# A copy moved ahead of a subtraction, and idle products between the first transposes

## The chip, the cores and the metric

The kernel runs on one core of a Trainium2 chip. A core has five engines with a queue of instructions each: TensorE (PE in the profile; its weight loads are listed apart as PEld) multiplies matrices, VectorE (DVE) and ScalarE (ACT) work on elements, GpSimd (POOL) does little here, and SyncE (SP) issues most DMA transfers. Products land in PSUM, which has eight banks of 128x512 float32; everything else that engines read lies in SBUF. The metric is the device time of one launch in microseconds (us). Less is better.

## The reference, cut to what matters

The program is a trunk of two layers over 1024 tokens of width 1024. Layer 0 mixes tokens with a gated MLP and a gated delta rule, layer 1 with differential attention; after each comes an MLP and a gated embedding. Only the first lines matter here:

```
hn = rms_norm(h, ln_mix_e[i])        # h is x at first
proj = hn @ w_in_e[i]
```

The norm divides each token's row by its root mean square and multiplies each of the 1024 columns by a gain, `ln_mix_e`. The product with `w_in_e` is the first product of the program.

## The kernel before

All activations are kept transposed: 128 columns of the model (one k of eight) by 512 tokens (one half of the sequence). A product in float32 is made of three in a faster 32-bit type: each operand is split into a high part (`hi`, the rounded value) and a low part (`lo`, the rest), and hi\*hi, lo\*hi and hi\*lo are summed in one PSUM bank.

For the first half of x the work before the first product is this:

- SyncE and ScalarE issue the loads: ScalarE first the gain's 8x128 values (L2063), then two pieces of x (L2050); SyncE, in turn, four pieces of each of x's two tiles and the pieces of the first weight (L103). A tile of x holds two blocks of 128 tokens; a piece is 256 of its columns, 256 KB, enough for two values of k. The loads use eight completion slots in turn, so the ninth is issued when the first slot's load has landed.
- TensorE runs five products of the identity with itself whose result nobody reads (`idle`, L2061, recorded at L78). Then it transposes the gain (into `pt`) and x, four 128x128 blocks for each k (recorded at L81), into a PSUM bank of 512 columns.
- ScalarE casts a weight piece to its high part (L226), and VectorE subtracts to get the low part (L227). Each weight piece of 256 rows becomes one 128x512 tile pair.
- VectorE copies the transposed gain from PSUM to `cols` (L2067). With it ScalarE evicts a transposed k as `hi` (L234) and VectorE makes `lo` (L235).
- `keep` copies the transposed x again, to `xt` (L880), and stores it to `h_dram` for the residual sum. `squares` (L885) is eight ScalarE instructions that sum x\*x by rows, for the norm. The division by the root mean square is done later, on the product's result.

The order on each engine's queue is fixed when the program is built: a planner replays the program against its own estimates of time and places each instruction; marks added by `Ordered.behind` only restrict that order. On the chip each queue then runs strictly as it was laid down. So an edit at the start also moves other instructions, by the planner's choice.

PSUM has two banks for each of the names `mm`, `aux`, `tr` and `sc`. Before the change the transposes of k take `aux`, `tr`, `sc` in turn, the idle products `tr`, the gain `aux`, and the first products `mm`.

Of the kernel before, what the change touches and what calls it, by code (L numbers as in the profile page):

```python
# [14 lines left out]
ALU = mybir.AluOpType  # L15
# [3 lines left out]
P = 128  # L19
# [4 lines left out]
HT = 512  # L24
# [8 lines left out]
MARKS = ((64, 50), (192, 144), (223, 168))  # L33
TAIL = 220
FILLA, FILLB, FILLC, FILLD = 62, 36, 28, 29
IDLE = 5

SYSTEMS = "k0 k1,k2 k3 d0,d1 s0,d2 s1 k4,d3 s2 k5,s3 k6 k7 d4,d5 s4,d6 s5,d7 s6,s7,,,,,".split(",")
FILLS = (20, 20, 20, 20, 26, 26, 28, 28)
# [2 lines left out]
def f32(ap):  # L42
    return ap.bitcast(F32)


class Ordered:
# [3 lines left out]
    def __init__(self, tc):  # L50
        self.tc, self.engine = tc, tc.nc.tensor
        self.fill = False
        self.start(0)
# [30 lines left out]
class Weight:  # L84
# [8 lines left out]
    def split(self, upto=None):  # L93
        while len(self.tiles) < min(upto or self.pieces, self.pieces):
            if len(self.raws) == len(self.tiles):
                self.load()
            self.tiles.append(self.T.parts(self.raws[len(self.tiles)], self.lo_engine))
# [19 lines left out]
class Trunk:  # L117
# [3 lines left out]
    def __init__(self, tc, ctx):  # L121
        self.tc, self.nc = tc, tc.nc
        nc = self.nc
        self.cp = ctx.enter_context(tc.tile_pool(name="const", bufs=1))
        self.wp = ctx.enter_context(tc.tile_pool(name="w", bufs=2))
        self.hp = ctx.enter_context(tc.tile_pool(name="hs", bufs=1))
        self.tp = ctx.enter_context(tc.tile_pool(name="tmp", bufs=TB))
        self.sp = ctx.enter_context(tc.tile_pool(name="small", bufs=2))

        self.rp = ctx.enter_context(tc.tile_pool(name="region", bufs=1))  # L130
        self.ps = ctx.enter_context(tc.tile_pool(name="ps", bufs=2, space=PSUM))
        self.wide = ("mm",)
        self.dp = ctx.enter_context(tc.tile_pool(name="dram", bufs=1, space=DRAM))
        self.n = self.turn = 0
        self.pe = Ordered(tc)
        self.ident = self.cp.tile([P, P], F32, name="ident")
        make_identity(nc, self.ident)
        self.ones = self.cp.tile([P, 1], F32, name="ones")
        nc.vector.memset(self.ones, 1.0)
        self.mhalf = self.cp.tile([P, 16], F32, name="mhalf")  # L140
        nc.vector.memset(self.mhalf, -0.5)

        warm = self.cp.tile([P, 1], F32, name="warm")
        nc.scalar.activation(warm, self.ones, AF.Tanh)
        self.hs = [None, None]

    def nm(self, s):
        self.n += 1
        return f"{s}_{self.n}"
# [74 lines left out]

    def split(self, src, hi, lo, lo_engine=None):
        self.nc.scalar.copy(hi, src)  # L226
        self.split_mark = (lo_engine or self.nc.vector).tensor_tensor(lo, src, f32(hi), ALU.subtract).ins.name  # L227
        return hi, lo

    def put_h(self, k, half, h, gain):  # L230
# [639 lines left out]
        self.pe.floor = None  # L870


    def load_x(self, rows, half, gain, h_dram):
        nc = self.nc
        ss = self.sp.tile([P, 2, 4], F32, tag="ssx", name=self.nm("ssx"))
        junk = self.slot("B", [P, 2, HT], F32, "junk")

        def keep(k, ps):
            xt = self.slot(f"c{k % 4}", [P, HT], F32, "xt")
            (nc.vector.tensor_copy if k % 4 else nc.scalar.copy)(xt, ps)  # L880
            nc.sync.dma_start(h_dram[k, :, half * HT : (half + 1) * HT], xt)

        def squares(i, u):
            for t in (2 * u, 2 * u + 1):
                inst = nc.scalar.activation(junk[:, t % 2], rows[t][:, i * HT : (i + 1) * HT], AF.Square, accum_out=ss[:, i, t : t + 1])  # L885
                if not half:
                    self.pe.behind(inst, marks[3 + 4 * i])

        late, marks = [], []
        for k in range(KT):  # L890

            ps = self.aux([P, HT], "aux" if half else ("aux", "tr", "sc")[k % 3], "aux")
            for t in range(4):
                self.pe.transpose(ps[:, t * P : (t + 1) * P], rows[t][:, k * P : (k + 1) * P], self.ident)
            marks.append(self.pe.mark)
            self.put_h(k, half, ps, gain[:, k : k + 1])
            late.append((k, ps))
            if half:
                keep(*late.pop())
                if k % 4 > 1:  # L900
                    squares(k // 4, k % 2)
            elif k > 3:
                keep(*late.pop(0))
            yield
        with contextlib.nullcontext() if half else self.tc.high_priority(EARLY):
            for i in range(0 if half else 4):
                squares(i // 2, i % 2)
            ms = self.sp.tile([P, 4], F32, tag="ms", name=self.nm("ms"))
            nc.vector.tensor_tensor(ms, ss[:, 0], ss[:, 1], ALU.add)
            nc.vector.tensor_scalar(ms, ms, 1.0 / D, EPS, ALU.mult, ALU.add)  # L910
            self.take_hs(half, ms)
        while late:
            keep(*late.pop(0))
        yield
# [1117 lines left out]
def trunk(tc, x, p, ln_mix_e, w_in_e, gmlp_v_gain, gmlp_ws, gmlp_bs, gdn_conv, gdn_a_log, gdn_dt_bias, gdn_out_gain,  # L2032
          w_out_e, ln_mix_o, w_qkv_o, attn_q_gain, attn_k_gain, diff_lambda, attn_sub_gain, w_out_o, ln_mlp, w_mlp1,
          w_mlp2, ln_ple, w_ple_gate, w_ple_proj, masks, out):
    with ExitStack() as ctx:
        T = Trunk(tc, ctx)
        nc = tc.nc
# [18 lines left out]
        cols = T.cp.tile([P, P], F32, name="cols")  # L2056
        vr = T.tmp()

        idle = T.aux([P, P], "tr", "idle")
        for _ in range(IDLE):  # L2060
            T.pe.matmul(idle, lhsT=T.ident, rhs=T.ident, start=True, stop=True)  # L2061
        first = Weight(T, [(w_in_e[0][:, 1536:1792], 0)], KT, 256)
        nc.scalar.dma_start(vr[0:8, 0:P], ln_mix_e[0].rearrange("(k p) -> k p", p=P))  # L2063
        x0 = rows(0)
        pt = T.aux_ps()
        T.pe.transpose(pt[:, 0:8], vr[0:8, 0:P], T.ident[0:8, 0:8])
        nc.vector.tensor_copy(cols[:, 0:8], pt[:, 0:8])  # L2067
        gain = [cols[:, i : i + 8] for i in (0, 8, 24, 40, 16, 32)]
        conv = cols[:, 48:96].rearrange("p (t m) -> p t m", m=12)
        lam_init = 0.8 - 0.6 * math.exp(-0.3)  # L2070
# [89 lines left out]
```

## Time and profile before

| what | value |
|---|---|
| time, median of 3 runs | 2512.21 us (2511.91 to 2512.52) |
| time of the profiled execution | 2513.05 us |
| its span, first to last instruction | 2511.1 us |
| busy: PE, DVE, ACT | 2495.5, 1810.3, 1307.4 us |
| first product of x and the weight, start | 9.30 us after the span's start |

In the timeline a row gives the start in us, the time it covers in us, the engine, the line, the operation, the tiles as output<-inputs, the shapes and a count of merged instructions; in brackets the idle time before it and what ended that. Starts count: on TensorE instructions overlap, so the pitch from start to start is what one costs. In the answers by stretch, each engine has its busy time with its count, and PEclk is the share of its clock that TensorE was granted. SPq and ACTq are the queues of those engines, where DMA issues stand.

### The profile page before, as it was taken

The numbers are of one execution on the slowest core, as the hardware profiler recorded it, in microseconds if no ns is written. First come the engines' busy times: TensorE is split into PE (matmuls) and PEld (weight loads), VectorE is DVE, ScalarE is ACT, GpSimd is POOL, SyncE is SP. The second block draws the span as 40 slices with busy tenths as digits, with TensorE's granted clock in tenths as the row PEclk, the third lists the DMA queues.
The fourth block names the chain that finished last, engine by engine and source line by source line (L and its number), as shares of the span: only waits on it lengthen the run. The fifth ranks groups of instructions, "written<-read, shape, count | busy, mean of one in ns | idle before, by whom it ended". The sixth has DMA issues, their size and how long they took to land.

```text
span 2511.1 us, 39815 instructions
## 1 busy us (share of the span) xinstructions
PE 2495.5 (99%) x13903; PEld 2138.6 (85%) x13903; DVE 1810.3 (72%) x3590; ACT 1307.4 (52%) x2654; POOL 258.1 (10%) x221
## 2 busy tenths in 40 slices
PE   9999999999999999999999999999999999999999
PEld 7898998888888888888999999988888888888887
DVE  7768665687666787656577777787887656788576
ACT  6635474554545444544465666655654555445452
POOL 0210220000000000000433333310000000000000
PEclk9999999999999999999999999999999999999999
DMA  7364436467557656544211111147466548666651
GB/s 237 121 187 106 134 114 197 130 194 257 181 173 268 229 175 210 189 130 136 88 46 52 47 43 43 60 142 256 157 217 229 191 164 293 201 187 203 198 176 63
DMA packets 314128, 403.19 MB, mean 161 GB/s; under 512 B 44772, under 2 KB 180936, under 8 KB 313928
## 3 DMA queue, kind: packets, MB, share of 16 engines
q1 hardware_dynamic: 313368, 400.13, 49.5%
q8 instruction: 109, 1.79, 0.3%
q14 instruction: 91, 0.75, 0.1%
q10 hardware_dynamic: 560, 0.53, 0.1%
HBM read 292.02 MB, written 108.53 MB: 160 GB/s over the span
## 4 chain that ended last, share of the span: by engine, by line
PE 95%; DVE 3%; issue 1%; ACT 0%; DMA 0%; POOL 0%; SPq 0%; DVEq 0%; ACTq 0%; POOLq 0%
PE mm L78 83%; PE po L78 3%; PE qk L78 2%; PE aux L78 2%; PE tr L81 2%; DVE lg L1092 0%; DVE t L1452 0%; PE pks L78 0%; PE pkq L78 0%; PE pvn L78 0%; PE aux L81 0%; PE pab L81 0%; DMA x<-in_x_dram 0%; DVE lg L1103 0%; ACT lg L1095 0%
## 5 line engine op out<-in xcount | busy, mean ns | idle before, releaser
L226 ACT CAST w<-raw 128x512 fp32r<-128x512 f32 x598 | 366.7, 618 | 474.9 <-PE mm L78 410.9
L78 PE MATMUL mm<-g,w 128*128 128x512 f32 x2592 | 603.0, 394 | 0.0
L78 PEld LDWEIGHTS mm<-g,w 128*128 128x128 f32 x2592 | 486.4, 188 | 115.5
L78 PE MATMUL mm<-hi,w 128*128 128x512 f32 x1728 | 554.3, 396 | 0.0
L227 DVE TENSOR_TENSOR w<-raw,w 128x512 fp32r<-128x512 f32 x534 | 365.0, 690 | 204.2 <-ACT w L226 190.6
L78 PE MATMUL mm<-w,hi 128*128 128x256 f32 (+2 forms) x2528 | 505.8, 295 | 0.7 <-DVE w L227 0.6
L78 PEld LDWEIGHTS mm<-w,hi 128*128 128x128 f32 x2528 | 400.7, 188 | 14.1 <-DVE w L227 0.8
L78 PEld LDWEIGHTS mm<-hi,w 128*128 128x128 f32 x1728 | 325.1, 189 | 73.4 <-ACT u L375 0.4
L78 PE MATMUL mm<-w,lo 128*128 128x256 f32 (+2 forms) x1264 | 369.6, 293 | 0.0
L78 PE MATMUL mm<-lo,w 128*128 128x512 f32 x864 | 340.7, 395 | 0.0
L78 PE MATMUL mm<-t,w 128*128 128x512 f32 x1152 | 271.7, 394 | 0.0
L78 PEld LDWEIGHTS mm<-t,w 128*128 128x128 f32 x1152 | 216.3, 188 | 51.1
L78 PEld LDWEIGHTS mm<-w,lo 128*128 128x128 f32 x1264 | 238.1, 188 | 5.4
L78 PEld LDWEIGHTS mm<-lo,w 128*128 128x128 f32 x864 | 162.6, 188 | 36.0 <-DVE lo L235 0.2
L264 POOL TENSOR_TENSOR r<-ms,mhalf 128x4 f32<-128x4 f32 x12 | 13.7, 1140 | 1511.0 <-DVE ms L262 1482.7
L227 DVE TENSOR_TENSOR g<-graw,g 128x512 fp32r<-128x512 f32 x216 | 147.4, 684 | 7.3 <-DMA gd<-g 2.8
L226 ACT CAST g<-graw 128x512 fp32r<-128x512 f32 x216 | 132.8, 617 | 26.3 <-DMA gd<-g 13.6
L1095 ACT ACTIVATE lg<-lg,nm 128x128 f32<-128x128 f32 (+7 forms) x128 | 99.4, 777 | 77.0 <-DVE nm L1092 70.3
L359 ACT ACTIVATE g<-g 128x512 f32<-128x512 f32 x100 | 63.0, 630 | 77.6 <-DVE g L293 77.4
L1092 DVE CUSTOM_DVE_ANT_0 lg<-qk,al 128x512 f32<-128x512 f32 (+3 forms) x128 | 74.9, 588 | 33.1 <-PE qk L78 30.3
L227 POOL TENSOR_TENSOR w<-raw,w 128x512 fp32r<-128x512 f32 x64 | 84.4, 1345 | 113.0 <-ACT w L226 64.8
L78 PE MATMUL mm<-ohi,w 128*128 128x512 f32 x256 | 85.2, 400 | 0.5 <-ACT ohi L1149 0.5
(358 smaller groups left out, 3539.1 us busy)
## 6 DMA issues: line engine op xcount, KB each, us to landing
raw<-in_w_mlp_dram SPq DMA_DIRECT2D x352, 256.0 KB, 3.4
graw<-gd SPq DMA_DIRECT2D x224, 256.0 KB, 2.7
gd<-g SPq DMA_DIRECT2D x192, 256.0 KB, 3.4
raw<-in_w_ple_gate_dram SPq DMA_DIRECT2D x76, 256.0 KB, 3.6
acc<-h_dram SPq DMA_DIRECT2D x64, 256.0 KB, 4.4
keep<-in_w_mlp_dram SPq DMA_DIRECT2D x64, 256.0 KB, 4.4
raw<-in_w_in_e_dram SPq DMA_DIRECT2D x60, 256.0 KB, 3.9
h_dram<-acc SPq DMA_DIRECT2D x48, 256.0 KB, 2.8
```

The source lines that it names most:

```text
L78: self._next(self.engine.matmul(*a, **k))
L81: self._next(self.engine.transpose(*a, **k))
L226: self.nc.scalar.copy(hi, src)
L227: self.split_mark = (lo_engine or self.nc.vector).tensor_tensor(lo, src, f32(hi), ALU.subtract).ins.name
L264: nc.gpsimd.tensor_tensor(r, ms, self.mhalf[:, 0:4], ALU.pow)
L359: nc.scalar.activation(g, src, AF.Relu)
L1092: nc.vector.tensor_tensor_reduce(out=lg[:, k0:k1], in0=ps[:, : k1 - k0], in1=al[:, u0 + k0 : u0 + k1], scale=-1.0, scalar=3.0e38 if c == 0 ...
L1095: nc.scalar.activation(lg[:, :n], lg[:, :n], AF.Exp, bias=nm[:, r, nch - 1 : nch], scale=-1.0, accum_out=me.sums[:, b, r : r + 1])
```

## The change

Five edits, all before or at the first product:

1. The copy of the gain to `cols` is named `first_lo`, and the first low part that is made after it in the program must be queued behind it on VectorE.
2. The idle products go from five to six, and write a bank of `sc` in place of `tr`.
3. The transposes of k = 0 and 1 are issued together: both k of x's first tile, five idle products, both k of the second tile, one idle product, and only then the rest.
4. The banks of the transposes are `aux`, `aux`, `tr`, `tr` in turn in place of `aux`, `tr`, `sc`.
5. From k = 4 on, the copy `keep` of k - 4 stands before the transposes of k, since these need its bank.

```
-IDLE = 5
+IDLE = 6
+WAIT = 5, 1
+BANKS = "aux", "aux", "tr", "tr"
...
     def split(self, src, hi, lo, lo_engine=None):
         self.nc.scalar.copy(hi, src)
-        self.split_mark = (lo_engine or self.nc.vector).tensor_tensor(lo, src, f32(hi), ALU.subtract).ins.name
+        inst = (lo_engine or self.nc.vector).tensor_tensor(lo, src, f32(hi), ALU.subtract)
+        if self.first_lo:
+            self.pe.behind(inst, self.first_lo)
+            self.first_lo = None
+        self.split_mark = inst.ins.name
         return hi, lo
...
+    def idle(self, n):
+        for _ in range(n):
+            self.pe.matmul(self.unread, lhsT=self.ident, rhs=self.ident, start=True, stop=True)
...
+        def turn(k, ps, ts):
+            for t in ts:
+                self.pe.transpose(ps[:, t * P : (t + 1) * P], rows[t][:, k * P : (k + 1) * P], self.ident)
+
+        def bank(k):
+            return self.aux([P, HT], "aux" if half else BANKS[k % 4], "aux")
+
+        early = []
+        if not half:
+            early = [bank(0), bank(1)]
+            for ts, n in ((range(2), WAIT[0]), (range(2, 4), WAIT[1])):
+                for k in range(2):
+                    turn(k, early[k], ts)
+                self.pe.floor = self.pe.mark
+                self.idle(n)
+                self.pe.floor = self.pe.mark
         for k in range(KT):
-
-            ps = self.aux([P, HT], "aux" if half else ("aux", "tr", "sc")[k % 3], "aux")
-            for t in range(4):
-                self.pe.transpose(ps[:, t * P : (t + 1) * P], rows[t][:, k * P : (k + 1) * P], self.ident)
+            if early:
+                ps = early.pop(0)
+            else:
+                if not half and k > 3:
+                    keep(*late.pop(0))
+                ps = bank(k)
+                turn(k, ps, range(4))
+                self.pe.floor = None
...
-            elif k > 3:
-                keep(*late.pop(0))
...
-        idle = T.aux([P, P], "tr", "idle")
-        for _ in range(IDLE):
-            T.pe.matmul(idle, lhsT=T.ident, rhs=T.ident, start=True, stop=True)
+        T.unread = T.aux([P, P], "sc", "idle")
+        T.idle(IDLE)
...
-        nc.vector.tensor_copy(cols[:, 0:8], pt[:, 0:8])
+        T.first_lo = nc.vector.tensor_copy(cols[:, 0:8], pt[:, 0:8]).ins.name
```

What the planner makes of it can be read in the built programs. On ScalarE, from the first weight cast on (k is counted from 0; one line is one or more instructions in their order):

```
before: cast piece 0 | hi k0, hi k1 | 2 squares of tile 0 | cast piece 1 | xt k0 | hi k2 | square | hi k3 | square
        | cast piece 2 | square | hi k4 | square | hi k5 | cast piece 3 | hi k6 | square | hi k7 | square | ...
after:  cast piece 0 | 2 squares of tile 0 | cast piece 1 | 2 squares of tile 1 | hi k0, hi k1 | cast piece 2 | hi k2
        | hi k3 | xt k0 | cast piece 3 | casts of the second weight's pieces 0 and 1 | hi k4 | hi k5
        | cast of its piece 2 | 2 squares | hi k6 | 2 squares | cast of its piece 3 | hi k7 | ...
```

The two squares of tile 0 read the columns of its first two pieces, those of tile 1 likewise. On VectorE the copy to `cols` stands before the first low part, and the low part of piece 1 before the first `lo`. On TensorE all transposes of k = 0 to 3 and the idle products stand before the first product, as before; the products of the second weight with k = 0 to 7 (24 of them) are spread between those of the first (48), where they stood behind them, and the first third-weight products come next where before 24 other products of the second came. On SyncE the first stores of `xt` go behind the loads of x's second half. Much later, at the end of the delta rule's solver, some ten groups of instructions change places on TensorE, VectorE and ScalarE; the rest of the program has the same order.

More of the change, by code (lines that the diff above doesn't have):

```diff
@@ L226, in split @@
         self.nc.scalar.copy(hi, src)
-        self.split_mark = (lo_engine or self.nc.vector).tensor_tensor(lo, src, f32(hi), ALU.subtract).ins.name
+        inst = (lo_engine or self.nc.vector).tensor_tensor(lo, src, f32(hi), ALU.subtract)
+        if self.first_lo:
+            self.pe.behind(inst, self.first_lo)
+            self.first_lo = None
+        self.split_mark = inst.ins.name
         return hi, lo
```

## The prediction

> **What bounds the kernel now.** First the page: busy shares and the chain of waits.
>
> ```profile
> span 2511.1 us, 39815 instructions
> PE 2495.5 (99%) x13903; PEld 2138.6 (85%) x13903; DVE 1810.3 (72%) x3590; ACT 1307.4 (52%) x2654; POOL 258.1 (10%) x221
> PE 95%; DVE 3%; issue 1%; ACT 0%; DMA 0%; POOL 0%; SPq 0%; DVEq 0%; ACTq 0%; POOLq 0%
> ```
>
> TensorE is busy for 99% of the span and makes 95% of the chain. So a delay of its first product stays to the end unless a later stall absorbs it, and later stalls are few. Next the chain in order of time over the first 40 us, cut to the start.
>
> ```profile
> 1.81 6.35 DMA x<-in_x_dram
> ...
> 8.20 1.45 PE aux L81 x8
> 9.65 3.10 PE mm L78 x8
> ```
>
> Until 8.2 us the chain waits for x's loads, then runs through transposes into products; from there TensorE never lets go. The change can win or lose only by when products start and how fast they then run. The speed is read from four stretches (busy us with counts for PE, PEld, DVE, ACT, POOL; then PEclk) and the timeline of TensorE.
>
> ```profile
> 2.03:5.44 3.41, 3.14 (x14) 2.37 (x13) 0.36 (x3) 0.91 (x2) 0.00 (x0) 1.00 0.95 219
> 5.44:8.85 3.41, 1.31 (x10) 1.01 (x11) 0.77 (x2) 0.99 (x2) 0.00 (x0) 1.00 1.09 365
> 8.85:12.27 3.42, 3.42 (x12) 2.80 (x11) 2.70 (x4) 3.42 (x9) 0.00 (x0) 0.50 1.10 348
> 12.27:15.68 3.41, 3.41 (x25) 2.94 (x24) 3.10 (x5) 3.41 (x10) 0.00 (x0) 1.00 1.09 365
> ```
> ```profile
> 1.42 2.50 PE L78 MATMUL idle<-ident 128*128 128x128 f32 x10 [1.42 <-POOL ident masks.py:199]
> ...
> 7.18 0.66 PE L81 MATMUL aux<-ident,x 128*128 128x128 f32 x4 [2.02 <-DMA x<-in_x_dram]
> 8.20 1.45 PE L81 MATMUL aux<-ident,x 128*128 128x128 f32 x8 [0.35 <-DMA x<-in_x_dram]
> 9.30 1.20 PE L78 MATMUL mm<-hi,w 128*128 128x512 f32 x2
> 10.30 0.63 PE L78 MATMUL mm<-lo,w 128*128 128x512 f32 x1
> 10.73 0.63 PE L78 MATMUL mm<-hi,w 128*128 128x512 f32 x1
> 11.16 0.63 PE L78 MATMUL mm<-lo,w 128*128 128x512 f32 x1
> ...
> 17.10 0.39 PE L78 MATMUL mm<-lo,w 128*128 128x512 f32 x1
> 17.33 0.39 PE L78 MATMUL mm<-hi,w 128*128 128x512 f32 x1
> ...
> 24.95 1.05 PE L78 MATMUL aux<-ident,r 128*128 128x128 f32 x8
> ```
>
> The granted clock sits at 0.50 from 8.85 to 12.27 and at 1.00 afterwards. At 0.50 products follow at 0.43 us (10.30, 10.73, 11.16), at 1.00 at 0.23 us (17.10, 17.33). The idle products ran at the slow pitch (ten instructions in 2.50 us against eight in 1.05 us at 24.95), so the 1.00 of the first row is no grant, only the absence of a record. The pattern: a stretch with 3.14 of 3.41 us busy is followed by 1.00, one with 1.31 by 0.50, one fully busy by 1.00.
>
> **Edit 1: the gain's copy first.** Three views carry it: VectorE, ScalarE, and three loads from SyncE's queue.
>
> ```profile
> 7.61 0.69 DVE L227 TENSOR_TENSOR w<-raw,w 128x512 fp32r<-128x512 f32 x1 [5.18 <-ACT w L226]
> 8.22 0.16 DVE L2067 COPY cols<-aux 128x8 f32<-128x8 f32 x1
> ```
> ```profile
> 6.96 0.62 ACT L226 CAST w<-raw 128x512 fp32r<-128x512 f32 x1 [4.01 <-DMA raw<-in_w_in_e_dram]
> 8.47 1.27 ACT L234 ACTIVATE hi<-aux,cols 128x512 fp32r<-128x512 f32 x2 [0.90 <-DVE cols L2067]
> 9.63 0.63 ACT L885 ACTIVATE junk<-x 128x512 f32<-128x512 f32 x1
> ...
> 10.24 0.62 ACT L885 ACTIVATE junk<-x 128x512 f32<-128x512 f32 x1
> ...
> 10.86 0.61 ACT L226 CAST w<-raw 128x512 fp32r<-128x512 f32 x1
> 11.36 0.59 ACT L880 COPY xt<-aux 128x512 f32<-128x512 f32 x1
> ```
> ```profile
> 8.17 0.37 SPq L103 DMA_DIRECT2D raw<-in_w_in_e_dram  x1
> 8.64 0.41 SPq L103 DMA_DIRECT2D raw<-in_w_in_e_dram  x1
> 9.39 0.37 SPq L103 DMA_DIRECT2D raw<-in_w_in_e_dram  x1
> ```
>
> Before, the copy waits behind a low part that waits for a load, and ScalarE's first `hi` waits for the copy until 8.47, though its transposes end at 7.85 (7.18 + 0.66). Taken alone, the copy made at about 4.7 us lets `hi` start at 7.9 and saves 0.57 us.
>
> But the built order of ScalarE has something else ahead of `hi`: cast, two squares, cast, two squares. I follow that queue. The first cast ends its issue at about 7.5. The squares read the second piece of x's first tile; that slot is free at 8.17, as SyncE's next issue shows, so they start at about 8.19. Two squares cost 1.23 (9.63 to 10.86 for two): 9.42. The next cast reads weight piece 1, landed by 9.39, so it does not wait: 0.50 (10.86 to 11.36): 9.92. The other tile's piece is there since 8.64; two squares: 11.15. Then `hi` k0 takes 0.69 and the product follows 0.07 later, as before (8.47 + 0.69 = 9.16, weight load 9.23): 11.91 against 9.23. **Later by 2.68 us.** No row suggests that an engine takes its queue out of order: `hi` stood idle behind nothing but its wait before.
>
> **Edits 2 and 3: idle products.** Seven more, two instructions each: 0.43 us each at the slow pitch, 0.22 at the fast. All lie in holes: the sixth delays the gain's transpose by 0.43 us, covered by the wait for x up to 7.18; the five run from about 5.1 to 6.4 (7.3 at worst, 0.1 late for x); the last lies before 8.20. With 11.91 as the start, none reaches the path: cost 0. If the squares did not hold `hi` back, the worst case would be 0.1 to 0.3 us. The new wait (k1's first transpose needs the bank that the gain's copy frees at 4.7) holds only transposes and idle products, all done before 7.2.
>
> Their effect on the clock: the stretch to 5.44 stays busy, so 1.00 holds to 8.85, as before. In 5.44:8.85 about 2.6 us are now busy against 1.31, so 1.00 may hold to 12.27 too, but only 0.36 us of products would use it. In 8.85:12.27 TensorE has the tail of the transposes (to 9.1) and 0.36 us of products: some 0.5 us busy, less than the 1.31 that was followed by 0.50. So 12.27 to 15.68 runs at 0.50. A slow stretch costs the share 1 - 0.23/0.43, or 46%: before 9.23 to 12.27, 3.04 us, 1.40 us lost; now 3.41 us, 1.57 lost. **Later by 0.17 us.**
>
> The Trainium skill (TensorE: Matmul & The Clock Gate, Part 1 and the section on HAM oscillation) says that the clock falls back after a window of about 3.4 us of idleness. The stretch of 5.44:8.85 was busy for 1.31 us and the clock still fell, so the trace asks for less than that; by the page the hole from 9.1 to 11.9 would be too short and the sum would be the first rival's.
>
> **Edits 4 and 5: banks.** With four banks in place of six, k4's transposes wait for ScalarE's `xt` of k0. By the queue: `hi` x2, cast, `hi` x2 from 11.15 (1.17 + 0.50 + 1.17 = 2.84) to 13.99, copy done at 14.6. TensorE comes to them after 14 products: one by 12.27, eight by 15.68, five more: 16.9. Margin 2.3 us, or 0.5 with a fast clock: cost 0. If the margin went, each us would be one us. The later `hi` of k4 (from 15.99 by the same count) is due at 20.9: margin 4.
>
> **Queues passed.** Four loads of x's second half pass the first two stores on SyncE; x comes about a us sooner, and its first transposes did not wait for it before: 0. The stores go later; the residual is read long after: 0. The 24 products of the second weight only change place with the first's: 0, as no operand is due before it is made by the counts above.
>
> **Later moves.** At the end of the solver groups change places, where these stalls lie:
>
> ```profile
> PE pd L78 <- DVE ring L1706: 1.0, 1, 1.0
> PE py L78 <- DVE xts L1796: 0.9, 2, 0.7
> ```
>
> The nearest prices are a stall of 0.7 us gone or one more like it: -0.7 to +0.7. I take 0, as most moves there are swaps of equals.
>
> **The sum:** +2.68 + 0.17 = +2.85 us. Against the profiled execution, 2513.05 us (span 2511.1 and 1.95 around it), 2515.9. That execution lies 0.84 us above the median of the runs shown, 2512.21, so for the median 2515.1.
>
> **The rivals.**
> 1. The clock stays at 1.00 once won. For it: the idle products nearly double the busy time of 5.44:8.85. Against: the hole of 2.8 us behind it. Then the start costs 2.68 and the slow 1.40 is saved: +1.28, 2513.5. The page named above would have it so.
> 2. Two slow stretches after the start, if products that still wait for `lo` don't fill the first. 2.68 + 2 x 1.57 - 1.40 = +4.42, 2516.6. Against: the fully busy 8.85:12.27, which won the clock at once.
> 3. Faster: ScalarE's squares do not hold `hi`, because their pieces and the casts come early enough or the queue runs otherwise. Then the product starts 0.57 sooner and, with the clock kept, 1.40 more is saved: -1.97, 2510.2. It decides if the first `hi` starts before the first square; the built order says no.
> 4. Slower by more than 0.2%: TensorE now reaches the third weight earlier in its order than before, after 72 products, at about 33.0 us (15.68 + 63 x 0.23 + 26 short ones x 0.11). This row shows when its first piece was castable before, after a wait:
>
> ```profile
> 29.16 0.62 ACT L226 CAST w<-raw 128x512 fp32r<-128x512 f32 x1 [1.09 <-DMA raw<-in_w_in_e_dram]
> ```
>
> It is ready at 29.8, 3.2 us ahead. The moved loads and stores would have to make it later by 3.2 + 2.2 us before the total passes +5.0, giving 2517.3 or more.
> 5. The change does nothing: no, the built order of ScalarE differs.
>
> **How the numbers follow.** Chances: the forecast 0.54, rival 1 0.17, rival 2 0.13, rival 3 0.05, rival 4 0.09, none of these 0.02. About 0.2%, 5.0 us, is what a measurement of this kernel can tell from no change; the forecast and rivals 1 to 3 lie inside it, with some of rival 2 beyond if the later moves cost. So same 0.85, slower 0.12, faster 0.03. The range goes from rival 1 less 0.7 (2512.8) to rival 2 with 0.7 more (2517.3). Forecast alone: 2514.4 to 2515.8.
>
> **What would show it.** The first `hi` behind four squares, at about 11.1 us, and the first product at about 11.9; the gain's copy before 5 us; 0.50 in some stretch after 12 us and products at 0.43 there; no idle time before k4's transposes; TensorE's third weight without a wait. It is wrong if `hi` comes before a square, if the clock holds, or if TensorE idles between 12 and 40 us.

## The result, and the profile after

The changed kernel took 2517.44 us (median of 21 runs, 2515.60 to 2519.36) against 2512.45 us (21 runs, 2509.96 to 2514.96) for the kernel before beside it: 1.0019 times as long, 95% interval 1.0013 to 1.0025. That is 5.0 us more. Repeated later, it was 2516.84 us (11 runs) against 2512.14: 1.0019 again, interval 1.0010 to 1.0027. Forecast were 2515.1 us and a range up to 2517.3. The loss has the right sign. As a time, the result lies 2.3 us above the forecast and 0.1 above the end of the range; as a loss against its own before, it is 5.0 us where 2.9 were forecast and the range went to 5.1 (2517.3 - 2512.21).

The first profiled execution of the changed kernel took 2516.42 us, 3.4 more than the one of before. First its page, then ScalarE and TensorE in its timeline.

```profile
span 2514.5 us, 39841 instructions
PE 2497.4 (99%) x13917; PEld 2140.2 (85%) x13917; DVE 1812.4 (72%) x3590; ACT 1307.6 (52%) x2654; POOL 257.7 (10%) x221
```
```profile
6.07 0.62 ACT L229 CAST w<-raw 128x512 fp32r<-128x512 f32 x1 [3.13 <-DMA raw<-in_w_in_e_dram]
7.94 0.63 ACT L896 ACTIVATE junk<-x 128x512 f32<-128x512 f32 x1 [1.26 <-DMA x<-in_x_dram]
...
9.18 0.60 ACT L229 CAST w<-raw 128x512 fp32r<-128x512 f32 x1
9.69 0.62 ACT L896 ACTIVATE junk<-x 128x512 f32<-128x512 f32 x1
...
10.92 1.24 ACT L241 ACTIVATE hi<-aux,cols 128x512 fp32r<-128x512 f32 x2
```
```profile
7.90 1.09 PE L83 MATMUL aux<-ident,x 128*128 128x128 f32 x8 [0.42 <-DMA x<-in_x_dram]
...
11.64 0.73 PE L80 MATMUL mm<-hi,w 128*128 128x512 f32 x2 [2.65 <-ACT hi L241]
12.43 0.74 PE L80 MATMUL mm<-lo,w 128*128 128x512 f32 x1
12.97 0.63 PE L80 MATMUL mm<-hi,w 128*128 128x512 f32 x1
13.40 0.63 PE L80 MATMUL mm<-lo,w 128*128 128x512 f32 x1
```

The first `hi` stands behind two casts and four squares until 10.92. TensorE has its transposes done at 9.0, waits 2.65 us for that `hi`, and starts its products at 11.64. The clock, by stretches (busy us and counts of PE, PEld, DVE, ACT, POOL; then PEclk):

```profile
5.69:9.10 3.41, 2.88 (x24) 2.45 (x23) 0.69 (x1) 1.78 (x5) 0.00 (x0) 1.00 1.05 343
9.10:12.52 3.42, 0.82 (x3) 0.39 (x3) 1.59 (x3) 3.42 (x10) 0.00 (x0) 1.00 1.10 356
12.52:15.93 3.41, 3.41 (x8) 2.67 (x9) 3.41 (x6) 3.34 (x7) 0.00 (x0) 0.50 1.09 359
```

The hole is followed by a stretch at 0.50, in which products follow each other at 0.43 us (12.97, 13.40). So far all is as forecast. The list of TensorE's waits (us in all, times, the longest in us) holds what was not. `xts` are copies out of PSUM that VectorE makes in the solver, and `py` the products that read them:

```profile
PE mm L80 <- ACT hi L241: 2.7, 1, 2.7
PE py L80 <- DVE xts L1826: 2.2, 2, 2.0
```

The waits for `xts` at the end of the solver grew from 0.9 to 2.2 us. VectorE around them, in the changed kernel and then in the kernel before:

```profile
201.32 0.69 DVE L230 TENSOR_TENSOR w<-raw,w 128x512 fp32r<-128x512 f32 x1 [2.22 <-ACT w L229]
201.93 0.69 DVE L1485 SCALAR_TENSOR_TENSOR qkv<-t,t 128x512 f32<-128x512 f32 x1
202.53 0.75 DVE L1482 SCALAR_TENSOR_TENSOR t<-cx,cols,t 128x512 f32<-128x512 f32 x1
203.20 0.69 DVE L230 TENSOR_TENSOR w<-raw,w 128x512 fp32r<-128x512 f32 x1
203.80 1.39 DVE L1826 COPY xts<-pz 32x512 f32<-32x512 f32 x2
...
207.47 1.40 DVE L1826 COPY xts<-pz 32x512 f32<-32x512 f32 x2
```
```profile
198.20 0.69 DVE L227 TENSOR_TENSOR w<-raw,w 128x512 fp32r<-128x512 f32 x1 [2.38 <-ACT w L226]
198.81 1.39 DVE L1796 COPY xts<-pz 32x512 f32<-32x512 f32 x2
...
203.09 1.40 DVE L1796 COPY xts<-pz 32x512 f32<-32x512 f32 x2
```

TensorE's `py` products in the changed kernel and before:

```profile
208.30 0.41 PE L80 MATMUL py<-xts,a 64*64 64x64 f32 x4 [1.97 <-DVE xts L1826]
```
```profile
203.91 0.41 PE L78 MATMUL py<-xts,a 64*64 64x64 f32 x4 [0.70 <-DVE xts L1796]
```

Before, one low part that waits for its cast stands ahead of the first two copies; now `qkv`, `t` and a second low part stand there too, 1.9 us of work. The copy that ends last ahead of the `py` products is the first of the next pair, at 207.47 (203.09 before). From pair to pair are 3.67 us now and 4.28 before, since `qkv` had stood in between; so 1.3 of the 1.9 us are left. The longest wait of TensorE, 0.70 us before, is now 1.97.

### The profile page after: what moved, and what is told of

It reads as the page before. It is cut to its first block, busy times and chain, and to the rows that moved or that the text cites. A ratio compares the mean times of both kernels' runs of the same rounds, so it can differ in the third digit from the quotient of the medians.

```text
span 2514.5 us, 39841 instructions
## 1 busy us (share of the span) xinstructions
PE 2497.4 (99%) x13917; PEld 2140.2 (85%) x13917; DVE 1812.4 (72%) x3590; ACT 1307.6 (52%) x2654; POOL 257.7 (10%) x221
## 3 DMA queue, kind: packets, MB, share of 16 engines
q8 instruction: 109, 1.79, 0.3%
## 4 chain that ended last, share of the span: by engine, by line
PE 89%; DVE 2%; ACT 0%; issue 0%; POOL 0%; DMA 0%; DVEq 0%; ACTq 0%; POOLq 0%
PE mm L80 77%; PE po L80 3%; PE qk L80 2%; PE aux L80 2%; PE tr L83 2%; DVE lg L1122 0%; PE pkq L80 0%; PE pks L80 0%; PE pvn L80 0%; PE pab L83 0%; DVE lg L1133 0%; ACT lg L1125 0%; PE pst L80 0%; PE pgm L80 0%; DVE w L230 0%
```

## The experiments

The theory: the loss is made at the front (the squares hold `hi`, and a 0.50 stretch follows the hole), with a second part from the order on VectorE at `xts`. The rivals: that the hold costs nothing by itself; that only the idle products cost; that the later order merely shifts a wait. Kernels measured together on one chip share the runs of the kernel before: the four from squares_alone to hi_first_wait51, the four from old_banks to late_order_pinned, and after_again with the last three. The interval of a ratio from 11 runs is 0.0009 to either side, some 2.2 us, so single microseconds rest on the traces.

| kernel | first product, us | 0.50 stretch behind the loads, us | first `pd` product, us | longest wait for `xts`, us | median, us | before beside it, us | ratio, interval |
|---|---|---|---|---|---|---|---|
| before | 9.30 | 8.85 to 12.27 | 105.5 | 0.70 | | | |
| after | 11.64 | 12.52 to 15.93 | 108.6 | 1.97 | 2517.44 | 2512.45 | 1.0019, 1.0013 to 1.0025 |
| after_again | 11.60 | 13.34 to 16.75 | 108.5 | 1.97 | 2516.84 | 2512.14 | 1.0019, 1.0010 to 1.0027 |
| squares_alone | 11.78 | 7.91 to 11.32 | 106.0 | 0.71 | 2512.78 | 2512.9 | 0.9999, 0.9990 to 1.0008 |
| no_idles | 9.01 | 8.57 to 11.98 | 105.4 | 0.72 | 2512.40 | 2512.9 | 0.9997, 0.9988 to 1.0006 |
| hi_first_wait41 | 8.72 | none | 104.4 | 0.67 | 2512.09 | 2512.9 | 0.9997, 0.9989 to 1.0006 |
| hi_first_wait51 | 8.55 | none | 104.1 | 0.70 | 2512.28 | 2512.9 | 0.9997, 0.9988 to 1.0006 |
| old_banks | 11.57 | none | 106.1 | 0.71 | 2511.84 | 2512.85 | 0.9997, 0.9988 to 1.0006 |
| hold_alone | 11.58 | 12.84 to 16.25 | 108.4 | 0.70 | 2515.02 | 2512.85 | 1.0009, 1.0000 to 1.0017 |
| hold_busy | 11.39 | none | 108.2 | 0.71 | 2515.90 | 2512.85 | 1.0014, 1.0005 to 1.0023 |
| late_order_pinned | 11.85 | none | 107.3 | none | 2513.92 | 2512.85 | 1.0006, 0.9997 to 1.0015 |
| edit1_alone | 8.95 | 8.07 to 11.48 | 104.9 | 0.74 | 2512.37 | 2512.14 | 1.0000, 0.9991 to 1.0009 |
| pins_alone | 9.03 | 7.77 to 11.18 | 104.9 | none | 2511.21 | 2512.14 | 0.9997, 0.9988 to 1.0006 |
| hi_first_pinned | 8.62 | none | 105.1 | none | 2510.88 | 2512.14 | 0.9995, 0.9986 to 1.0003 |

The `pd` products are the solver's, shortly before its first stall: up to them the front's loss can be read. The front varies from one execution to the next: pins_alone has the same instructions as before up to there and was 0.6 us earlier (104.9 against 105.5).

**squares_alone**: the kernel before with the four squares of k0 to k3 marked to stand ahead of `hi` of k0, and nothing else. (In the trace `hi` of k1 runs between them, at 9.26, and `hi` of k0 behind the fourth, at 11.05.)

```
+        if not half:
+            for u in range(2):
+                squares(0, u)
+            self.hi_behind = self.square_mark
```

> The kernel before with the four squares of the first columns marked to stand ahead of the first product's hi on ScalarE, and nothing else; no more idle products, the banks of before, the solver's order of before. Theory: first product at about 11.5 to 12.0 us, two slow stretches in all, 2.5 to 3.3 us above before (ratio 1.0010 to 1.0013), and no longer wait for xts in the solver. Rival (products wait for something else, the squares are hidden): within 1 us of before.

The expected loss did not come: 2512.78 against 2512.9. Yet the hold is there. TensorE in the timeline:

```profile
7.97 3.58 PE L81 MATMUL aux<-ident,x 128*128 128x128 f32 x16 [0.62 <-DMA x<-in_x_dram]
11.78 0.73 PE L78 MATMUL mm<-hi,w 128*128 128x512 f32 x2 [0.22 <-ACT hi L235]
```

The first product starts at 11.78, but TensorE idles only 0.22 us before it: it has 16 transposes to run, those of k4 and k5 among them, and it passes its 0.50 stretch with them. The first product is 2.48 us later than in before, `pd` only 0.5. The transposes of k4 and k5 stood behind the first product in before: 8 x 0.11 = 0.9 us are won back with them. The 0.50 stretch, which cost before about 1.40 us of its products by the count of the prediction, now lies on the transposes. So a late `hi` is nearly no loss here for two reasons: needed work fills the hole, and the slow clock falls into it.

**no_idles**: the changed kernel with the idle products of before.

```
-IDLE = 6
-WAIT = 5, 1
+IDLE = 5
+WAIT = 0, 0
```

> The changed kernel with five idle products at the start and none between the transposes. Built so, ScalarE's first hi stands directly behind the first cast, ahead of all squares, and the solver's order is that of before. Theory (the idle products make the planner put four squares and a cast ahead of hi, and that is the loss): the first product starts near 8.0 to 8.7 us, one stretch at 0.50 as before, and the time is 0.5 to 1 us under before (ratio 0.9996 to 0.9998). Rival (the banks, the new order of the transposes or the early copy cost the time, not the squares): it stays 2 us or more above before (ratio 1.0008 or more).

First product at 9.01, later than expected, but no hold: ScalarE runs `hi` directly behind the first cast. The time is that of before (the expected gain is too small to be told from it), so the rival is out. The hold is written in no edit; it is how the planner answers the idle products.

**hi_first_wait51, hi_first_wait41**: the changed kernel, its idle products kept (five or four, and one), with the squares and the second cast marked behind `hi` of k0 and k1.

```
+        if self.casts == 2:
+            self.pe.behind(cast, self.early_hi)
...
-                    self.pe.behind(inst, marks[3 + 4 * i])
+                    self.pe.behind(inst, his[1 + 2 * i])
```

> The same with five idle products in the first group, as in the change; the solver's order then is nearly that of the changed kernel. Front as in the run with four. Theory that the changed order in the solver costs by itself (a wait for xts of about 2.0 us where before has 0.7): 0.7 to 1.5 us above the run with four, with that wait in the trace. Rival (that wait comes from the later start, not from the order): the same time as the run with four within 0.5 us and a wait for xts of 0.7.

> The changed kernel with the squares and the second cast marked to stand behind hi of k1 on ScalarE, and four idle products in place of five in the first group, so that the solver's order is that of before. Theory: first product at 8.0 to 8.7 us, no stretch at 0.50 behind it or one that the products fill only in part; 1 to 2.5 us under before (ratio 0.9990 to 0.9996). Rival (the idle products themselves, by delaying transposes, or the clock cost the time): first product at 9.5 us or later, ratio 1.0005 or more.

First product at 8.55 and 8.72, no 0.50 stretch behind it, and yet no gain over before that the runs resolve: the medians are 0.6 and 0.8 us lower, where 1 to 2.5 were expected of the run with four. Their order at `xts` turned out to be that of before, so they say nothing on the late order. Where the front's gain ends is seen on VectorE of hi_first_wait51:

```profile
22.69 0.69 DVE L895 COPY xt<-aux 128x512 f32<-128x512 f32 x1 [2.87 <-DMA h_dram<-xt]
```

The copy to `xt` waits 2.87 us for the store of an earlier one: the buffers of `xt`, freed by stores, are the next bound, and TensorE waits 0.50 us behind them, at 23.53.

**old_banks**: the changed kernel with edits 4 and 5 undone.

```
-BANKS = "aux", "aux", "tr", "tr"
+BANKS = "aux", "tr", "sc"
...
-                if not half and k > 3:
-                    keep(*late.pop(0))
...
+            elif k > 3:
+                keep(*late.pop(0))
```

> After with the third part of the change undone: three banks in turn for x's transposes, and the copy that keeps a tile behind the next tile's transposes, as in before. ScalarE still has four squares and a cast ahead of the first hi. Theory (the hold costs what the hole in TensorE's work costs): TensorE fills the hole with the transposes of k4 and k5, the first product still starts at about 11.7 us, the products behind it run without the later gap for k4 and k5, and the time is 2512.5 to 2514.3, that is +0 to +1.5 us. Rival (the hold of hi is paid in full whatever stands in the hole): first product at about 11.7 and 2515 us or more.

2511.84 us: the rival (the hold is paid in full) is out, and the loss is even smaller than the theory's. ScalarE still has both casts and four squares ahead of `hi`, but TensorE fills the hole:

```profile
9.65 0.44 PE L83 MATMUL aux<-ident,x 128*128 128x128 f32 x2 [0.49 <-DMA x<-in_x_dram]
10.41 0.87 PE L83 MATMUL aux<-ident,x 128*128 128x128 f32 x6 [0.32 <-DMA x<-in_x_dram]
11.57 0.73 PE L80 MATMUL mm<-hi,w 128*128 128x512 f32 x2 [0.29 <-ACT hi L241]
```

Its products also have no 0.50 stretch, which cost before about 1.40 us. So the hold costs nothing measurable on balance: 2.27 us of later start stand against 0.9 us of transposes and this stretch. Edits 4 and 5 are undone together; their shares are not told apart.

**hold_alone**: the changed kernel with the squares issued as in squares_alone, which leaves TensorE's front as in after (ScalarE's second cast stands behind all four squares) and gives VectorE the order of before at `xts`. **hold_busy**: the same with ten idle products behind the transposes of k3.

```
+                if not half and k == 3:
+                    self.pe.floor = self.pe.mark
+                    self.idle(10)
+                    self.pe.floor = None
```

> After, with the four squares of the first pair of tiles issued directly and the first hi marked behind them; the front's order on ScalarE and TensorE is that of after, while VectorE's order at the solver's copies of xts is that of before. Theory: first product at about 11.6 us, second 0.50 stretch of the clock, waits for xts at about 0.9 us, and +2.0 to +3.0 us: 2514.8 to 2516.0. Rival (later order worth nothing): as after, 2517 or more.

> The kernel with the hold alone, and ten idle products behind the transposes of the fourth tile of x, in the hole ahead of the first product. Theory (the clock's second stretch at 0.50 follows the hole): the first product stays at about 11.6 us, no stretch at 0.50 follows it, and the time is 1.3 to 1.7 us under the kernel with the hold alone: 2513.2 to 2514.6. Rival (the stretch at 0.50 comes whatever stands in the hole, or its products wait for something else anyway): the same as the hold alone within 0.4 us, 2514.8 to 2516.0.

hold_alone came out as the theory had it: 2515.02 us, first product at 11.58, waits for `xts` as before. Against old_banks, measured beside it, the ranges of the runs do not overlap (2513.65 to 2515.74 against 2511.46 to 2512.61), and both start their products at the same time. So it is the banks, with the order of `keep` that goes with them, that make the hold cost. In the traces `pd` starts 2.3 us later than with the old banks. That is about what two things make: eight transposes behind the hole and not in it (8 x 0.11 = 0.9 us) and the 0.50 stretch of 3.41 us (46% of it, 1.57). Where the time goes fits: matched product by product, hold_alone is 1.5 us behind old_banks at 15.7 us, with most of the stretch past, 2.2 behind at 22 us, with the transposes past, and it stays there up to `pd`, although the built orders of the two differ in places up to 75 us.

hold_busy missed its expectation: 2515.90 us, no better than hold_alone. The clock did as expected, 1.00 throughout, but the time won was not kept. TensorE's list of waits has the reason:

```profile
PE aux L83 <- DVE xt L895: 1.3, 1, 1.3
PE mm L80 <- ACT hi L242: 0.4, 1, 0.4
```

At 43.0 us its transposes wait 1.26 us for a copy to `xt`, which frees their bank. The copy is late above all because VectorE stood still for a load of a gain:

```profile
39.50 0.23 DVE L1997 TENSOR_SCALAR carved<-carved 128x128 f32<-128x128 f32 x1 [3.22 <-DMA carved<-in_gdn_out_gain_dram]
...
42.18 0.68 DVE L895 COPY xt<-aux 128x512 f32<-128x512 f32 x1
```

In hold_alone the same instruction runs at 39.50 too, after a wait of 0.27 us. Up to there hold_busy is 1.8 us ahead, product by product; at `pd` 0.2 are left. So here a load that lands no sooner takes the gain. That the median is 0.9 us above hold_alone's is within the runs' intervals and stays unexplained.

**late_order_pinned**: the changed kernel, with a mark that holds `qkv`, `t` and the second low part behind the copies to `xts`. **pins_alone**: the same mark in the kernel before.

```
+                if p == 0:
+                    self.pin, self.lows = inst.ins.name, 0
...
+        if self.pin:
+            self.lows += 1
+            if self.lows > 1:
+                self.pinned(inst)
+                self.pin = None
```

> After's front is unchanged; only VectorE's order at the solver's copies of xts is set back to that of before (the copies ahead of the second low part, of qkv and of t). Theory (front hold, plus a late order on VectorE that costs of itself): the first product stays at about 11.6 us and the clock's second 0.50 stretch at about 12.5 to 15.9, the waits of TensorE for xts fall from 2.2 to about 0.9 us, the pair of profiles shrinks from +3.4 to about +2.1 us over before, and the median lies at 2515.0 to 2516.3, some 1.3 us under after. Rival (the whole loss is made at the front and the later wait only shifts): no gain against after, 2517 or more, and the ratio to before stays at 1.0019.

> Before with one thing changed, far behind the front: the order on VectorE at the solver's copies of xts (the copies ahead of qkv, t and the second low part). Theory (that order is worth its own time, whatever the front does): the waits for xts fall from 0.9 to 0.3 us or less, and the time is 0.6 to 1.2 us under before: 2511.3 to 2512.3. Rival (what is not waited for there is waited for later): within 0.3 us of before, 2512.3 or more.

late_order_pinned is 2513.92 us, better than the theory's 2515.0 to 2516.3; the rival (2517 or more) is out. The front is as late as in after (first product at 11.85), and the waits for `xts` are gone altogether, not only back at 0.9. Two things helped: the pins go beyond the order of before, and this execution had no 0.50 stretch behind the hole. The trace gives prices for the front. The kernel of after_again has the same instructions up to the solver and a 0.50 stretch, and comes to `pd` 1.3 us later (108.55 against 107.25) although its products start 0.25 sooner: 1.5 us for the stretch. The kernel old_banks, also without a stretch, comes to `pd` 1.1 us sooner (106.12) and starts its products 0.28 sooner: 0.9 us for the transposes behind the hole. pins_alone, at 2511.21 against 2512.14, has the expected size (0.9 us), which the runs can't separate from zero. Its trace shows the wait gone:

```profile
202.54 2.52 PE L78 MATMUL py<-xts,a 64*64 64x64 f32 x64
```

All 64 products of `xts` run in one piece with no wait ahead of them. Beside edit1_alone, which comes to `pd` at the same time, pins_alone is 1.0 us ahead behind these products and 1.5 at the end of the span (2508.9 against 2510.4), so in these two executions nothing of it is lost again.

**edit1_alone**: the kernel before with the first edit only.

```
+        if self.first_lo:
+            self.pe.behind(inst, self.first_lo)
+            self.first_lo = None
...
+        T.first_lo = nc.vector.tensor_copy(cols[:, 0:8], pt[:, 0:8]).ins.name
```

> Before with the first part of the change alone: the copy of the norm's columns ahead of the first weight's low part on VectorE; no idle products, no other banks. Theory: the copy is done by about 5 us, the first hi no longer waits for the columns and starts at 7.5 to 8.2 us, the first product at 8.4 to 9.0 us in place of 9.30, and the time is 0.3 to 0.9 us under before: 2511.6 to 2512.6. Rival (the first product waits for x and not for the columns): no difference, 2512.4 to 2513.2, with the first product at 9.2 us or later.

2512.37 against 2512.14. The time does not decide: it lies in the range of the theory and next to that of the rival, and the first product, at 8.95, in that of the theory. The timeline does, and for the rival's cause. `hi` starts early, and the product waits for something else:

```profile
6.79 1.26 ACT L239 ACTIVATE hi<-aux,cols 128x512 fp32r<-128x512 f32 x2
```
```profile
7.63 1.67 PE L81 MATMUL aux<-ident,x 128*128 128x128 f32 x8 [0.66 <-DMA x<-in_x_dram]
8.95 1.20 PE L78 MATMUL mm<-hi,w 128*128 128x512 f32 x2
```

`hi` of both k is done by 8.05, but TensorE's order has eight transposes of k2 and k3 ahead of the first product, and these wait for x until 7.63. pins_alone, whose front is that of before, starts at 9.03, so the edit alone is worth no more than 0.1 us beside it.

**after_again**: the changed kernel itself, with no edit.

> The changed kernel once more, for a second profiled execution and for times beside the others of this call. Theory (hold of the first hi, a 0.50 stretch behind or ahead of it, and the late order on VectorE): first product at 11.4 to 11.9 us, longest wait for xts 1.9 to 2.1 us, profile +3 to +5 us over the profile of before, median +4.5 to +5.5 us over before. If the median's +5.0 was an accident of the chip it was timed on, it comes out at +3.0 to +4.0 us.

The median's loss is confirmed (+4.7 us), and so are both causes: first product at 11.60, longest wait for `xts` 1.97. Its span is 2515.4 us, 4.3 over before's.

**hi_first_pinned**: both causes taken away, the marks of hi_first_wait51 and of late_order_pinned together.

> The changed kernel with both causes taken away: the squares and the second cast marked behind the first two tiles' hi, and the pinned order on VectorE at the copies of xts. Theory (the two add up): first product at 8.4 to 8.9 us, waits for xts 0.3 us or less, profile 2 to 4 us under that of before, and a median 1.3 to 2.2 us under before: 2510.5 to 2511.6. Rival (the front's gain is lost again further back): no faster than the front's repair alone, 2512.0 to 2512.6.

2510.88 us (2510.03 to 2511.77) lies clear of after_again, measured beside it (2516.33 to 2518.18), so the loss of the change is undone. Against before it is 0.9995 with an interval that takes in 1: it is the fastest median here, but not shown to beat before, and its span is 1.3 us under before's where 2 to 4 were expected. The front gave little: `pd` starts at 105.1, since on VectorE the copies to `xt` wait for stores again, for 3.40 us, and TensorE behind them for 1.44.

```profile
23.68 0.69 DVE L905 COPY xt<-aux 128x512 f32<-128x512 f32 x1 [3.40 <-DMA h_dram<-xt]
```

## Why the prediction was right and wrong

**Right: the hold.** Forecast were a first `hi` behind four squares at about 11.1 and a first product at about 11.9; they came at 10.92 and 11.64. Nearly all of the 0.27 is the first square's, at 7.94 in place of 8.19. Rival 3 (squares don't hold `hi`) is out. At `pd` after is 3.1 us late where 2.85 was forecast, though start and clock as they came make only 2.6 (2.68 - 0.27 + 0.17); the other 0.5 us are not assigned.

**Right here, by chance of the phase: the clock.** The 0.50 stretch was forecast for 12.27 to 15.68 and came at 12.52 to 15.93. In the second execution it came at 13.34 to 16.75, and late_order_pinned, with the same front, had none:

```profile
7.60:11.02 3.42, 1.66 (x15) 1.42 (x13) 0.69 (x1) 2.88 (x8) 0.00 (x0) 1.00 1.08 357
11.02:14.43 3.41, 2.53 (x10) 1.79 (x11) 2.60 (x5) 3.41 (x9) 0.00 (x0) 1.00 1.10 348
```

The edges here are those of the trace's own clock record, which begins at 7.60 and next falls at 2509.57. So rival 1 (the clock holds) is what one of four traces with this hole did (after, after_again and hold_alone have the 0.50 stretch); the prediction took the edges of one profiled execution as if they were fixed. Rival 2 (two slow stretches) was not seen in any trace. The Trainium skill (TensorE: Matmul & The Clock Gate, Part 1) calls the window free-running, not reset by a kernel's start. The traces agree: with the same instructions the edge lies at 8.85 in before and at 7.77 in pins_alone.

**Wrong: the banks at cost 0.** The margin of 2.3 us for k4's transposes held, and no wait appeared. But the step asked only whether the new wait would be late, not what TensorE could have done in the hole with the old banks. old_banks shows that the hold with the old banks costs nothing that can be measured, the clock's gain included; hold_alone shows it at +2.2 us with the new ones. So the forecast's 2.68 + 0.17 for the front was about the right size for a reason that it named only by half: the late `hi` and the banks together.

**Wrong: the later moves at 0, with 0.7 as their bound.** This is the step that put the time above the forecast. "Most moves there are swaps of equals" was not true of VectorE, where 1.9 us of work went ahead of the first copies and 1.3 us of delay reached the copy that TensorE waits for. The trace shows it as 1.27 us of wait (0.70 to 1.97). By medians the difference between after_again and hold_alone, each against its own before, is 4.7 - 2.2 = 2.5 us. In the traces after's span exceeds hold_alone's by 1.5 us in one execution, of which 0.2 are there ahead of `xts`, and by 2.4 in the other, where TensorE also waits 0.71 us for a low part at 301.90. Before has such a wait too (0.59 us at 297.44), the first execution of after has not. So the late order is worth about 1.3 us, and whether the rest belongs to it is open.

**Half right: edit 1's saving of 0.57 us, taken alone.** The wait of `hi` for the copy went, as said, but it was not alone on the path: with the copy early, the first product stands behind TensorE's own order and x's loads (edit1_alone).

**The rest.** The built orders of before and after differ on TensorE, VectorE and ScalarE in more places up to 74 us than the section on the change names; between 12 and 74 us TensorE waits for none of it in the trace. Edits 2 and 3 cost nothing by their own time, as said; the idle products cost by what the planner made of them. TensorE did not wait for the third weight, so rival 4's mechanism did not happen, although its time did. Rival 5 (no effect) is out.

## What to carry to other kernels

Where a planner lays the queues, read every engine's built order down to the last difference and price each one at the wait nearest to it; an edit in the first ten microseconds moved a copy at 204. A late operand costs the hole that it leaves and what the clock does behind it: before pricing it, ask what else the waiting engine could run, and whether the same change took that work away. A gain at the start is kept only until the next thing is late, here the `xt` tiles waiting for their stores at 23 us, or a load that lands at 39.5.

## What had not been expected of the hardware

The clock does not need an idle stretch to fall, as the prediction already suspected. In the traces stretches of 3.41 us in which TensorE was busy for 0.82, 1.08, 1.19, 1.29, 1.31, 1.40, 1.43 or 1.69 us were followed by 0.50, and those with 1.79 us or more by 1.00, over the whole of every trace. The Trainium skill (TensorE: Matmul & The Clock Gate, Part 1) has the clock fall after a window of some 3.4 us of idleness; here the measurement differs. The 1.79 us are those of the wait for `xts` in after_again:

```profile
204.49:207.90 3.41, 1.79 (x8) 1.13 (x6) 3.30 (x5) 0.00 (x0) 0.00 (x0) 1.00 0.88 221
207.90:211.32 3.42, 2.85 (x66) 2.63 (x67) 3.30 (x8) 1.62 (x3) 0.00 (x0) 1.00 0.87 188
```

Near half of a stretch the two overlap: 1.66 us was followed by 1.00 (late_order_pinned, above), 1.69 us by 0.50 (after_again):

```profile
9.93:13.34 3.41, 1.69 (x6) 1.12 (x7) 2.29 (x4) 3.41 (x9) 0.00 (x0) 1.00 1.10 348
13.34:16.75 3.41, 3.41 (x10) 2.56 (x9) 3.41 (x7) 2.48 (x5) 0.00 (x0) 0.50 1.08 365
```

And a stretch of nothing but transposes wins the clock: in squares_alone 7.91 to 11.32 was busy for 3.35 us with 16 transposes, and the next stretch was granted 1.00.

```profile
7.91:11.32 3.41, 3.35 (x16) 3.19 (x16) 1.35 (x2) 3.30 (x10) 0.00 (x0) 0.50 1.09 359
11.32:14.74 3.42, 3.20 (x16) 2.39 (x15) 2.98 (x5) 3.42 (x7) 0.00 (x0) 1.00 1.10 350
```
